# Mixture-of-experts weights: four split feature blocks and one plain fp32 block stationary, the rest streaming in pieces of 256, and a ring of ten weight tiles

## The chip, the cores and the metric

The kernel runs on one core of a Trainium2 chip. The metric is the device time of one execution in microseconds, as the median of several runs; lower is better. The core has a matrix engine (TensorE: PE in the profile, its weight loads PEld), a vector engine (VectorE, DVE), an activation engine (ScalarE, ACT), a general engine (GpSimd, POOL), a queue engine (SyncE, SP) that issues most transfers, and 16 DMA engines. Each engine runs its own instructions in order; engines wait for each other by semaphores. TensorE writes to PSUM, which DVE and ACT read.

A matmul on TensorE has two operands. The stationary one is loaded into the array first, with as many columns as the output has partitions; the moving one streams through it column by column. In the profile's rows a matmul reads `out<-moving,stationary`.

## The reference, cut to what matters

Two layers of a hybrid encoder. Each ends in a mixture of experts: 16 experts, each of which takes its 66 tokens of 528 (D_MODEL = 1024, EXPERT_FF = 1408). All of it is float32.

```python
def expert_choice_ffn(u, router, w1, w3, w2):
    B, L, D = u.shape
    cap = EC_FACTOR * L // N_EXPERTS
    aff = jax.nn.softmax(jnp.einsum("bld,de->ble", u, router).astype(jnp.float32), axis=-1)
    gates, idx = lax.top_k(jnp.swapaxes(aff, 1, 2), cap)
    xs = jax.vmap(lambda ub, ib: ub[ib])(u, idx)
    hid = jax.nn.silu(jnp.einsum("becd,edf->becf", xs, w1)) * jnp.einsum("becd,edf->becf", xs, w3)
    ys = jnp.einsum("becf,efd->becd", hid, w2) * gates[..., None].astype(u.dtype)
    return jax.vmap(lambda yb, ib: jnp.zeros((L, D), yb.dtype).at[ib].add(yb))(ys, idx)
```

## The kernel before

Everything ahead of the experts (input projection, three head groups, output projection, routing) is the same in both kernels. The change lies in the experts' stage, which runs once per layer.

**Weights.** Per expert, w1, w3 and w2 each come as four tiles of 128 partitions x 2816 (1408 KB); 12 tiles per expert, 384 in the program. `wtile` (L1100 issues it on SP) takes tiles from a ring of RA + RB = 9: five in one pool, four in another. A slot is loaded again when its last reader is through. One manual dependence holds a tile of the first fill back until the first expert's tokens are gathered.

**Split precision.** The fast matmul format fp32r doesn't keep all of float32, so each operand is split in a high and a low part, and three products are summed: high x high, low x high, high x low. `halve` splits a stretch of a weight tile: ACT copies it to fp32r (`wh`, L1111), DVE subtracts to get the rest (`wl`, L1112). Both land in rings of four buffers, so the splitting engines can be up to four pieces ahead of TensorE. For w1 and w3 a piece is one k: 128 rows of the weight matrix times all 1408 features, 8 pieces each. For w2 a tile is cut in two pieces of 1280 or 1536.

**Up (w1, w3).** `up_tile` (matmuls at L1156) multiplies one piece. Features 0 to 1023 stream as two stretches of 512 with the 66 tokens stationary, three matmuls each, into `h1a`/`h1b` (w3: `h3a`/`h3b`). Features 1024 to 1407 are three blocks of 128 that are stationary themselves; the tokens stream, high and low side by side (132 columns) against `wh` and high alone (66) against `wl`, into `h1T`/`h3T`. The wide and the short matmuls are issued in turn.

**Gate, down, order.** `gate_up` and `gated` form silu(w1 x) * (w3 x) on DVE and ACT, `hidden` transposes the row part back with eight TensorE transposes (`pth`) and splits it; `down` (L1217) streams w2 in stretches of 512 or 256 into `py`, `yo` scales by the gate (L1221), and an indirect DMA adds it into `hbuf` (L1222). `operands` transposes the next expert's tokens (`ptx`, eight transposes) and splits them (`xx`). The loop is a software pipeline: w1 of expert e, then w2 of expert e-1, then w3 of expert e; `hidden` of the previous expert follows the first tile of w1, `operands` of the next the second tile of w3. A scheduler orders each engine's instructions from this; the order within an engine is fixed when the program is built.

Of the kernel before, what the change touches and what calls it, by code (L numbers as in the profile page):

```python
# [23 lines left out]
D = 1024  # L24
# [22 lines left out]
RA, RB = 5, 4  # L47
WT = 2816

# [56 lines left out]
def body(ctx: ExitStack, tc: tile.TileContext, a, out, dbg=None, depth=DEPTH, stop=None):  # L106
# [104 lines left out]
    for l in range(depth):  # L211
# [879 lines left out]
        with tc.tile_pool(name="mw", bufs=1, reuse_waits="tile") as mw, \  # L1091
# [15 lines left out]
            def halve(w, lo, hi):  # L1107
                n = hi - lo
                wh = mhl.tile([128, 1536], F32R, name="wh", bufs=4)[:, :n]
                wl = mhl.tile([128, 1536], F32R, name="wl", bufs=4)[:, :n]  # L1110
                A.activation(wh, w[:, lo:hi], AF.Copy)  # L1111
                splits.append(behind(V.tensor_sub(wl, w[:, lo:hi], wh.bitcast(F32)),  # L1112
                                     chosen if len(splits) < 4 else None))
                return wh, wl

            def tokens(e):
                xg = mo.tile([128, D], F32, name="xg", bufs=3)
# [6 lines left out]
            def operands(xg):  # L1124
                xx = mo.tile([128, KT, 2, CAP], F32R, name="xx")
                for q in range(2):
# [6 lines left out]
                    A.activation(xx[:, ks, 0], src, AF.Copy)  # L1133
                    V.tensor_sub(xx[:, ks, 1], src, xx[:, ks, 0].bitcast(F32))  # L1134
                return xx

            def up_tile(src, xx, ps_, q):
# [20 lines left out]
            def halves(pT):  # L1158
                return pT[:, :6 * CAP].rearrange("p (b x n) -> p b n x", b=3, x=2)

            def gate_up(ps_):
                pa, pb, pT = ps_
                tt = mo.tile([128, 1024], F32, name="tt")
                tT = mo.tile([128, 2, 3, CAP], F32, name="tT")
                V.tensor_reduce(tT[:, 0], halves(pT), axis=AX.X, op=OP.add)
                for c, p in ((0, pa), (1, pb)):
                    t_ = tt[:CAP, c * 512:(c + 1) * 512]
                    A.activation(t_, p[:CAP, :], AF.Tanh, scale=0.5)
                    V.scalar_tensor_tensor(t_, t_, 1.0, p[:CAP, :], op0=OP.add, op1=OP.mult)
                A.activation(tT[:, 1], tT[:, 0], AF.Tanh, scale=0.5)  # L1170
                V.scalar_tensor_tensor(tT[:, 0], tT[:, 1], 1.0, tT[:, 0], op0=OP.add, op1=OP.mult)
                return tt, tT

            def gated(ts, ps_):
                (tt, tT), (pa, pb, pT) = ts, ps_
                for c, p in ((0, pa), (1, pb)):
                    t_ = tt[:CAP, c * 512:(c + 1) * 512]
                    V.tensor_mul(t_, t_, p[:CAP, :])
                V.tensor_reduce(tT[:, 1], halves(pT), axis=AX.X, op=OP.add)
                V.tensor_mul(tT[:, 0], tT[:, 0], tT[:, 1])  # L1180

            def hidden(ts):
# [3 lines left out]
                for c in range(3):  # L1186
                    if c < 2:
# [160 lines left out]
```

## Time and profile before

| what | value |
|---|---|
| device time, median of 3 runs | 2734.44 us (2730.94 to 2737.09) |
| profiled execution | 2737.51 us, its span 2735.7 us |
| busy over the span | PE 2518.9 us (92%), DVE 2170.6 (79%), ACT 1604.4 (59%), POOL 441.3 (16%) |
| weight tiles of the experts | 384 of 1408 KB, median 10.9 us from issue to landing |
| experts' stage | about 640 to 1355 us and 1985 to 2705 us |

The page cuts the span in 40 slices; in the two stretches of the experts' stage PE, DVE and DMA stand at 9 (90% or more) in every slice and ACT at 8. Elsewhere no engine is full for long. So the stage is read by itself: by windows of one expert, by the start times of TensorE's matmuls, and by groups of instructions that keep shapes apart. A matmul's duration includes its way through the array and overlaps the next one, so spacing is taken from start to start.

### The profile page before, as it was taken

How to read it: one execution, taken by the hardware profiler on the slowest of the kernel's cores; microseconds unless marked ns; L12 is line 12 of the kernel's file. 1: busy time of each engine (PE TensorE's matmuls, PEld its weight loads, DVE VectorE, ACT ScalarE, POOL GpSimd, SP SyncE). 2: the span in 40 equal slices, each digit the busy share in tenths (PEclk: the TensorE clock that was granted, in tenths of full speed). 3: DMA queues.
4: the chain of work that ended last, by engine and by line, in shares of the span. 5: the costliest groups of instructions: out<-in, count | busy, mean ns of one | idle time of the engine just before them, and what ended most of it. 6: DMA issues, size and time to landing. Idle time of an engine off the chain costs nothing.

```text
span 2735.7 us, 46610 instructions
## 1 busy us (share of the span) xinstructions
PE 2518.9 (92%) x18586; PEld 1981.8 (72%) x18586; DVE 2170.6 (79%) x3293; ACT 1604.4 (59%) x2107; POOL 441.3 (16%) x545
## 2 busy tenths in 40 slices
PE   7899999786999999999788899998689999999995
PEld 6778786565777777778587787755467787877783
DVE  3557667758999999999735676687589999999995
ACT  3324334425888888788542343344268888888884
POOL 3113322213000000000121133241120000000000
PEclk9878999997999999999997789999889999999998
DMA  3101101148999999999420111022499999999993
GB/s 129 47 24 60 37 25 51 64 172 312 408 400 405 403 399 409 397 412 404 174 77 32 40 44 49 13 73 93 148 358 393 413 397 411 399 409 401 407 402 117
DMA packets 84682, 643.30 MB, mean 235 GB/s; under 512 B 12592, under 2 KB 13040, under 8 KB 35312
## 3 DMA queue, kind: packets, MB, share of 16 engines
q1 hardware_dynamic: 75936, 618.16, 57.0%
q0 software_dynamic: 8528, 22.15, 3.3%
q8 instruction: 146, 2.39, 0.4%
q14 instruction: 72, 0.59, 0.1%
HBM read 617.05 MB, written 19.40 MB: 233 GB/s over the span
## 4 chain that ended last, share of the span: by engine, by line
PE 41%; DVE 5%; issue 2%; ACT 2%; DMA 1%; POOL 0%; DVEq 0%; SPq 0%; ACTq 0%; POOLq 0%
PE py L1217 9%; PE pj L288 5%; PE h1a L1156 4%; PE h3a L1156 3%; PE h1b L1156 3%; PE h3b L1156 3%; PE h1T L1156 1%; PE h3T L1156 1%; PE po L1026 1%; PE po L730 1%; DMA hbuf<-yo,idx 1%; PE S L898 1%; PE pl L473 1%; PE up L307 1%; PE py L563 0%
## 5 line engine op out<-in xcount | busy, mean ns | idle before, releaser
L1112 DVE TENSOR_TENSOR wl<-w,wh 128x1408 fp32r<-128x1408 f32 (+2 forms) x768 | 1212.7, 1617 | 59.9 <-ACT wh L1111 35.3
L1111 ACT ACTIVATE wh<-w 128x1408 fp32r<-128x1408 f32 (+2 forms) x768 | 1042.7, 1378 | 196.9 <-PE py L1217 78.5
L1217 PE MATMUL py<-wh,hh 128*66 128x512 f32 (+1 forms) x768 | 289.2, 377 | 4.3 <-ACT hh L1197 4.3
L1217 PE MATMUL py<-wh,hl 128*66 128x512 f32 (+1 forms) x768 | 288.7, 376 | 0.8 <-DVE hl L1198 0.8
L1217 PE MATMUL py<-wl,hh 128*66 128x512 f32 (+1 forms) x768 | 288.4, 375 | 0.0
L1222 POOL DMA_INDIRECT hbuf<-yo,idx x32 | 54.9, 1714 | 1190.0 <-ACT yo L1221 1076.6
L1156 PE MATMUL h1a<-wh,xx 128*66 128x512 f32 x512 | 186.1, 414 | 1.1 <-DVE xx L1134 1.1
L1156 PE MATMUL h3a<-wh,xx 128*66 128x512 f32 x512 | 182.8, 408 | 0.0
L1156 PE MATMUL h1b<-wh,xx 128*66 128x512 f32 x512 | 176.3, 410 | 0.0
L1156 PE MATMUL h3b<-wh,xx 128*66 128x512 f32 x512 | 174.7, 407 | 0.0
L1156 PE MATMUL h1T<-xx,wh 128*128 128x132 f32 x768 | 172.1, 224 | 0.0
L1156 PE MATMUL h3T<-xx,wh 128*128 128x132 f32 x768 | 171.3, 223 | 0.0
L288 PE MATMUL pj<-uh,wh 128*128 128x264 f32 (+1 forms) x896 | 166.5, 314 | 5.2 <-ACT kS L344 5.0
L288 PE MATMUL pj<-ul,wh 128*128 128x264 f32 (+1 forms) x896 | 162.2, 313 | 0.0
L288 PE MATMUL pj<-uh,wl 128*128 128x264 f32 (+1 forms) x896 | 155.6, 303 | 0.0
L1217 PEld LDWEIGHTS py<-wh,hh 128*66 128x66 f32 x768 | 105.2, 137 | 64.1 <-ACT hh L1197 4.5
L1217 PEld LDWEIGHTS py<-wl,hh 128*66 128x66 f32 x768 | 105.1, 137 | 60.6 <-issue 1.0
L1156 PE MATMUL h1T<-xx,wl 128*128 128x66 f32 x768 | 148.9, 194 | 0.0
L1156 PEld LDWEIGHTS h3T<-xx,wh 128*128 128x128 f32 x768 | 146.6, 191 | 2.7
L1156 PEld LDWEIGHTS h1T<-xx,wh 128*128 128x128 f32 x768 | 148.3, 193 | 0.0
L1156 PE MATMUL h3T<-xx,wl 128*128 128x66 f32 x768 | 148.3, 193 | 0.0
L1217 PEld LDWEIGHTS py<-wh,hl 128*66 128x66 f32 x768 | 105.3, 137 | 59.1 <-DVE hl L1198 1.5
(444 smaller groups left out, 5061.9 us busy)
## 6 DMA issues: line engine op xcount, KB each, us to landing
w<-in_e_w SPq DMA_DIRECT2D x384, 1408.0 KB, 10.9
w<-in_w_in SPq DMA_DIRECT2D x56, 512.0 KB, 3.5
wo<-in_w_out SPq DMA_DIRECT2D x16, 512.0 KB, 3.5
h<-hbuf SPq DMA_DIRECT2D x12, 512.0 KB, 4.7
swp<-raw SPq DMA_DIRECT2D x64, 66.0 KB, 2.0
h<-in_x SPq DMA_DIRECT2D x8, 512.0 KB, 7.2
hbuf<-h SPq DMA_DIRECT2D x8, 512.0 KB, 2.8
ubuf<-u POOLq DMA_DIRECT2D x8, 512.0 KB, 4.6
```

Source lines behind the costliest of these rows:

```text
L288: T.matmul(p[:M, c, :HL], ww[:, k, :M], uu[:, k, c * HL:(c + 1) * HL], start=(n == 0), stop=(n == 23))
L307: T.matmul(p[:, c, :HL], lhsT, rhs[:, c * HL:(c + 1) * HL], start=True, stop=True)
L473: T.matmul(pl[:, b, :], flat(BC[m][:, jm[m]]), az[:, m].rearrange("p x q n -> p (x q n)"), start=True, stop=True)
L730: T.matmul(o_, qd[d][hc(h), j * CH:(j + 1) * CH], kv[hc(h), d, j, :], start=False, stop=(d == 1), tile_position=(32 * h, 64 * (h % 2)))
L898: behind(T.matmul(p[:R], qk[0, h][:, qo:qo + R], qk[1, h][:, c, NM:], start=True, stop=True), mark)
L1026: T.matmul(p[:R, c, :], mm[:, k, o:o + R], ww[:, k, c * 512:(c + 1) * 512], start=(n == 0), stop=(n == 23))
L1111: A.activation(wh, w[:, lo:hi], AF.Copy)
L1112: splits.append(behind(V.tensor_sub(wl, w[:, lo:hi], wh.bitcast(F32)), chosen if len(splits) < 4 else None))
L1156: T.matmul(o_, l_, r_, start=s0, stop=s1)
L1217: T.matmul(py[:CAP, c, d0:d0 + n], x[:, kk, :], ww[:, at0 - lo:at0 - lo + n], start=(kk == 0 and i_ == 0), stop=(kk == FK - 1 and i_ == 2))
L1222: G.indirect_dma_start(out=hbuf[:, :], out_offset=bass.IndirectOffsetOnAxis(ap=idx[:CAP, e:e + 1], axis=0), in_=yo[:CAP], in_offset=None, ...
```

## The change

- Features 0 to 767 stream (FROW = 768), in stretches of 256: three stretches, nine matmuls per piece where there were six of 512.
- Features 768 to 1279 are four stationary split blocks (there were three). One of them goes to the free half of `h1b`/`h3b`.
- Features 1280 to 1407 are one stationary block in plain fp32: the weight tile itself is the operand, not split, against unsplit tokens `xf` (two more ACT copies per expert). So a tile of w1 or w3 has a third reader, TensorE.
- `halve` splits 1280 columns per piece of w1 or w3. Its buffers are 1280 wide (1536 before), so a w2 tile is cut in three pieces (1024, 1024, 768) and not two.
- Within a piece short and wide matmuls still take turns; in the last piece the wide ones go first.
- The epilogues read one bank more: a reduce and two small operations more in `gate_up` and in `gated`. The row part has six blocks to transpose and not eight.
- The ring has ten tiles (RB = 5). `xg` has two buffers (three), `yo` one (two).

```diff
-RA, RB = 5, 4
+RA, RB = 5, 5
 WT = 2816
+FROW, FCOL = 768, 1280
+NT = (FF - FROW) // 128
+WSPL = FCOL
...
-                wh = mhl.tile([128, 1536], F32R, name="wh", bufs=4)[:, :n]
-                wl = mhl.tile([128, 1536], F32R, name="wl", bufs=4)[:, :n]
+                wh = mhl.tile([128, WSPL], F32R, name="wh", bufs=4)[:, :n]
+                wl = mhl.tile([128, WSPL], F32R, name="wl", bufs=4)[:, :n]
...
-                xg = mo.tile([128, D], F32, name="xg", bufs=3)
+                xg = mo.tile([128, D], F32, name="xg", bufs=2)
...
                     A.activation(xx[:, ks, 0], src, AF.Copy)
+                    A.activation(xf[:, ks], src, AF.Copy)
...
-                    wh, wl = halve(w, j * FF, (j + 1) * FF)
+                    wh, wl = halve(w, j * FF, j * FF + FCOL)
...
-                    for c, p in ((0, pa), (1, pb)):
+                    for c in range(FROW // 256):
+                        p = (pa, pb)[c // 2][:CAP, c % 2 * 256:c % 2 * 256 + 256]
                         for i, (x, ww) in enumerate(((0, wh), (1, wh), (0, wl))):
-                            rows.append((p[:CAP, :], xx[:, kk, x], ww[:, c * 512:(c + 1) * 512],
-                                         first and i == 0, last and i == 2))
-                    for b in range(3):
-                        f = slice(1024 + 128 * b, 1152 + 128 * b)
-                        cols.append((pT[:, b * 2 * CAP:(b + 1) * 2 * CAP], wh[:, f],
-                                     xx[:, kk].rearrange("p x n -> p (x n)"), first and b == 0, False))
-                        cols.append((pT[:, b * 2 * CAP:b * 2 * CAP + CAP], wl[:, f], xx[:, kk, 0], False, last and b == 2))
-                    for pair in zip(rows, cols):
+                            rows.append((p, xx[:, kk, x], ww[:, c * 256:c * 256 + 256],
+                                         first and i == 0 and c == 0, last and i == 2 and c == 1))
+                    for b in (0, 1, 2, 3) if first else (1, 2, 3, 0):
+                        f = slice(FROW + 128 * b, FROW + 128 + 128 * b)
+                        p, at0 = (pb, 256) if b == 0 else (pT, (b - 1) * 2 * CAP)
+                        cols.append((p[:, at0:at0 + 2 * CAP], wh[:, f],
+                                     xx[:, kk].rearrange("p x n -> p (x n)"), first and b < 2, False))
+                        cols.append((p[:, at0:at0 + CAP], wl[:, f], xx[:, kk, 0], False, last and b == 0))
+                    cols.insert(6, (pT[:, 6 * CAP:7 * CAP], w[:, j * FF + FCOL:(j + 1) * FF], xf[:, kk], False, last))
+                    for pair in zip(rows, cols) if last else zip(cols, rows):
...
-                    mid = WT // 2 // 512 * 512 + (512 if q % 2 == 0 else 256)
-                    for lo, hi in ((0, mid), (mid, WT)):
+                    cuts = (0, 1024, 2048, WT) if q % 2 == 0 else (0, 768, 1792, WT)
+                    for lo, hi in zip(cuts, cuts[1:]):
...
-                yo = mo.tile([128, D], F32, name="yo")
+                yo = mo.tile([128, D], F32, name="yo", bufs=1)
```

The order on TensorE within a piece of w1, before; a row is line, operation, `out<-moving,stationary` and output partitions x columns:

```order
L1156 MATMUL h1a<-wh,xx 66x512
L1156 MATMUL h1T<-xx,wh 128x132
L1156 MATMUL h1a<-wh,xx 66x512
L1156 MATMUL h1T<-xx,wl 128x66
L1156 MATMUL h1a<-wl,xx 66x512
L1156 MATMUL h1T<-xx,wh 128x132
L1156 MATMUL h1b<-wh,xx 66x512
L1156 MATMUL h1T<-xx,wl 128x66
```

And the last twelve matmuls of such a piece in the changed kernel:

```order
L1165 MATMUL h1T<-xx,wl 128x66
L1165 MATMUL h1a<-wh,xx 66x256
L1165 MATMUL h1T<-xx,wh 128x132
L1165 MATMUL h1a<-wh,xx 66x256
L1165 MATMUL h1T<-xx,wl 128x66
L1165 MATMUL h1a<-wl,xx 66x256
L1165 MATMUL h1T<-xf,w 128x66
L1165 MATMUL h1b<-wh,xx 66x256
L1165 MATMUL h1b<-xx,wh 128x132
L1165 MATMUL h1b<-wh,xx 66x256
L1165 MATMUL h1b<-xx,wl 128x66
L1165 MATMUL h1b<-wl,xx 66x256
```

Each wide matmul still has a short one ahead of it; the seventh row is the new plain fp32 matmul, which reads the weight tile.

On DVE at the end of w1 and the start of w2, before (`wl` rows are splits, 1408 wide for w1, 1536 or 1280 for w2):

```order
L1112 TENSOR_TENSOR wl<-w,wh 128x1408 x2
L1112 TENSOR_TENSOR wl<-w,wh 128x1536
L1112 TENSOR_TENSOR wl<-w,wh 128x1280 x2
L1169 SCALAR_TENSOR_TENSOR tt<-tt,h1a 66x512
L1165 TENSOR_REDUCE tT<-h1T 128x198
L1112 TENSOR_TENSOR wl<-w,wh 128x1536
L1169 SCALAR_TENSOR_TENSOR tt<-tt,h1b 66x512
L1171 SCALAR_TENSOR_TENSOR tT<-tT 128x198
L1112 TENSOR_TENSOR wl<-w,wh 128x1536
```

and in the changed kernel:

```order
L1115 TENSOR_TENSOR wl<-w,wh 128x1280 x2
L1115 TENSOR_TENSOR wl<-w,wh 128x1024 x2
L1115 TENSOR_TENSOR wl<-w,wh 128x768
L1171 TENSOR_REDUCE tT<-h1T 128x198
L1184 SCALAR_TENSOR_TENSOR tt<-tt,h1a 66x512
L1169 TENSOR_REDUCE tT<-h1b 128x66
L1188 SCALAR_TENSOR_TENSOR tT<-tT,h1T 128x66
L1115 TENSOR_TENSOR wl<-w,wh 128x768
L1184 SCALAR_TENSOR_TENSOR tt<-tt,h1b 66x256
L1187 SCALAR_TENSOR_TENSOR tT<-tT 128x264
L1115 TENSOR_TENSOR wl<-w,wh 128x1024 x4
```

Four small operations now stand between the third and the fourth split of w2, where there were two.

On SP at the first fill of the ring, layer 0, before (numbers tell the tiles apart; DMASW is the gather of the first tokens):

```order
L1100 DMA w_7029<-in_e_w3 128x2816 [waits PE_49]
L1100 DMA w_7078<-in_e_w3 128x2816 [waits DMAHW4_49,Pool_49]
L1100 DMA w_7205<-in_e_w1 128x2816 [waits DVE_49]
L1100 DMA w_7112<-in_e_w3 128x2816 [waits DMAHW6_49,DMASW6_49]
L1100 DMA w_7153<-in_e_w1 128x2816 [waits DMAHW7_49]
```

and in the changed kernel:

```order
L1103 DMA w_7095<-in_e_w3 128x2816 [waits PE_49]
L1103 DMA w_7159<-in_e_w3 128x2816 [waits DMAHW4_49,Pool_49]
L1103 DMA w_7205<-in_e_w3 128x2816
L1103 DMA w_7260<-in_e_w1 128x2816 [waits DMAHW6_49,DMASW6_49]
L1103 DMA w_7322<-in_e_w1 128x2816 [waits DMAHW7_49]
```

The third of these tiles waited for DVE to split a first tile; it now waits for nothing and is issued with the two ahead of it. The next one still waits for the gather.

## Rows read from the trace of the kernel before

**Rows 1.** Windows: length, busy time (instructions) of PE, PEld, DVE, ACT, POOL, clock, DMA share, GB/s
```profile
921.55:965.78 44.23, 44.23 (x281) 34.41 (x280) 42.90 (x38) 35.97 (x34) 2.97 (x2) 1.00 1.01 406
1173.00:1217.00 44.00, 44.00 (x281) 34.28 (x280) 42.66 (x38) 35.75 (x34) 1.72 (x1) 1.00 1.01 411
```

**Rows 2.** Timeline of PE, one expert: start us, us, what, shape, count
```profile
921.55 0.40 PE L1156 MATMUL h3a<-wh,xx 128*66 128x512 f32 x1
...
928.51 0.69 PE L1129 MATMUL ptx<-cst,xg 66*128 66x66 f32 x8
929.00 0.43 PE L1156 MATMUL h3a<-wh,xx 128*66 128x512 f32 x1
...
950.50 0.42 PE L1217 MATMUL py<-wh,hh 128*66 128x512 f32 x1
...
965.78 0.39 PE L1156 MATMUL h3a<-wh,xx 128*66 128x512 f32 x1
```

**Rows 3.** Timeline of PE within a piece of w1
```profile
900.12 0.22 PE L1156 MATMUL h1T<-xx,wh 128*128 128x132 f32 x1
...
900.42 0.19 PE L1156 MATMUL h1T<-xx,wl 128*128 128x66 f32 x1
900.45 0.42 PE L1156 MATMUL h1b<-wh,xx 128*66 128x512 f32 x1
900.71 0.22 PE L1156 MATMUL h1T<-xx,wh 128*128 128x132 f32 x1
```

**Rows 4.** Timeline of PE in w2: last of 512 columns, first of six of 256
```profile
909.54 0.39 PE L1217 MATMUL py<-wl,hh 128*66 128x512 f32 x1
909.77 0.28 PE L1217 MATMUL py<-wh,hh 128*66 128x256 f32 x1
...
910.48 0.40 PE L1217 MATMUL py<-wh,hh 128*66 128x512 f32 x1
```

**Rows 5.** Plain fp32 elsewhere: L1049 by source, then timelines of PEld and PE
```profile
L1049 PE MATMUL plg<-rt,hT x160: 176/262/263, 548.8 to 1968.0; 128*128 128x16 f32 x128, 128*16 128x16 f32 x32
...
271.97 0.19 PEld L288 LDWEIGHTS pj<-ul,wh 128*128 128x128 f32 x1
272.07 0.98 PEld L550 LDWEIGHTS pu<-xs,zz 128*128 128x128 f32 x8
...
272.19 1.00 PE L550 MATMUL pu<-xs,zz 128*128 128x64 f32 x8
...
273.66 0.33 PE L557 MATMUL pS<-uv,bct 128*64 128x64 f32 x2
```

**Rows 6.** Groups by shape, 921.55 to 965.78, DVE then ACT: busy us, mean ns
```profile
L1112 DVE TENSOR_TENSOR wl<-w,wh 128x1408 fp32r<-128x1408 f32 x17 | 27.2, 1620 | 1.3 <-PE h3T L1156 0.6 <-ACT wh L1111 0.4
L1112 DVE TENSOR_TENSOR wl<-w,wh 128x1280 fp32r<-128x1280 f32 x4 | 5.8, 1482 | 0.0
...
L1133 ACT ACTIVATE xx<-ptx 128x264 fp32r<-128x264 f32 x2 | 0.7, 378 | 0.0
```

**Rows 7.** Timeline, fourth split of a w2: its DVE end, its first matmul
```profile
909.03 1.74 DVE L1112 TENSOR_TENSOR wl<-w,wh 128x1536 fp32r<-128x1536 f32 x1
...
911.86 0.39 PE L1217 MATMUL py<-wh,hh 128*66 128x512 f32 x1
```

**Rows 8.** Weight tiles by source, 700 to 1275: landing after issue
```profile
DMA to landing us min/median/max: 8.4/11.0/15.0
```

**Rows 9.** Timeline at the stage's start: first gather, first transposes
```profile
627.75 6.10 POOL L1118 DMA_INDIRECT xg<-ubuf,idx  x1 [4.38 <-DVE idx L1078]
...
637.69 1.14 PE L1129 MATMUL ptx<-cst,xg 66*128 66x66 f32 x8 [11.15 <-DMA xg<-ubuf,idx]
```

**Rows 10.** Timeline of PE, two fp32r streams before plain fp32 on 64 rows
```profile
89.51 0.40 PE L288 MATMUL pj<-uh,wh 128*128 128x264 f32 x2
89.90 0.31 PE L697 MATMUL pk<-vtC,km 64*32 64x64 f32 x7
```

More of the change, by code (lines that the diff above doesn't have):

```diff
@@ L1125, in operands @@
                 xx = mo.tile([128, KT, 2, CAP], F32R, name="xx")
+                xf = mo.tile([128, KT, CAP], F32, name="xf")
                 for q in range(2):
@@ L1133, in operands, with up_tile @@
                     A.activation(xx[:, ks, 0], src, AF.Copy)
+                    A.activation(xf[:, ks], src, AF.Copy)
                     V.tensor_sub(xx[:, ks, 1], src, xx[:, ks, 0].bitcast(F32))
-                return xx
-            def up_tile(src, xx, ps_, q):
+                return xx, xf
+            def up_tile(src, xs_, ps_, q):
+                xx, xf = xs_
                 w = wtile(src)
@@ L1155, in up_tile, with gathered @@
+                    cols.insert(6, (pT[:, 6 * CAP:7 * CAP], w[:, j * FF + FCOL:(j + 1) * FF], xf[:, kk], False, last))
+                    for pair in zip(rows, cols) if last else zip(cols, rows):
                         for o_, l_, r_, s0, s1 in pair:
                             T.matmul(o_, l_, r_, start=s0, stop=s1)
-            def halves(pT):
-                return pT[:, :6 * CAP].rearrange("p (b x n) -> p b n x", b=3, x=2)
-            def gate_up(ps_):
[L1162 to L1171, printed above, removed]
+            def gathered(dst, ps_):
+                pa, pb, pT = ps_
+                V.tensor_reduce(dst[:, 0], pb[:, 256:256 + 2 * CAP].rearrange("p (x n) -> p n x", x=2),
+                                axis=AX.X, op=OP.add)
+                V.tensor_reduce(dst[:, 1:4], pT[:, :6 * CAP].rearrange("p (b x n) -> p b n x", b=3, x=2),
+                                axis=AX.X, op=OP.add)
+                return pT[:, 6 * CAP:7 * CAP]
@@ new lines, in rows_of @@
+            def rows_of(ps_):
+                return ((slice(0, 512), ps_[0][:CAP, :]), (slice(512, FROW), ps_[1][:CAP, :FROW - 512]))
+            def gate_up(ps_):
+                tt = mo.tile([128, FROW], F32, name="tt")
+                tT = mo.tile([128, 2, NT, CAP], F32, name="tT")
+                own = gathered(tT[:, 0], ps_)
+                for c, p in rows_of(ps_):
+                    A.activation(tt[:CAP, c], p, AF.Tanh, scale=0.5)
+                    V.scalar_tensor_tensor(tt[:CAP, c], tt[:CAP, c], 1.0, p, op0=OP.add, op1=OP.mult)
+                A.activation(tT[:, 1, :4], tT[:, 0, :4], AF.Tanh, scale=0.5)
+                A.activation(tT[:, 1, 4], own, AF.Tanh, scale=0.5)
+                V.scalar_tensor_tensor(tT[:, 0, :4], tT[:, 1, :4], 1.0, tT[:, 0, :4], op0=OP.add, op1=OP.mult)
+                V.scalar_tensor_tensor(tT[:, 0, 4], tT[:, 1, 4], 1.0, own, op0=OP.add, op1=OP.mult)
@@ L1172, in gate_up @@
                 return tt, tT
             def gated(ts, ps_):
[L1175 to L1180, printed above, removed]
+                tt, tT = ts
+                for c, p in rows_of(ps_):
+                    V.tensor_mul(tt[:CAP, c], tt[:CAP, c], p)
@@ L1182, in hidden @@
+                own = gathered(tT[:, 1], ps_)
+                V.tensor_mul(tT[:, 0, :4], tT[:, 0, :4], tT[:, 1, :4])
+                V.tensor_mul(tT[:, 0, 4], tT[:, 0, 4], own)
             def hidden(ts):
@@ L1185, in hidden @@
                 hl = mo.tile([128, FK, CAP], F32R, name="hl")
-                for c in range(3):
-                    if c < 2:
+                for k0, n in ((0, 4), (4, 2), (6, NT)):
+                    if k0 < 6:
                         pt = t_tile("pth")
-                        for k in range(4):
-                            kk = 4 * c + k
-                            T.transpose(pt[:, k * CAP:(k + 1) * CAP], tt[:CAP, kk * 128:(kk + 1) * 128],
+                        for k in range(n):
+                            T.transpose(pt[:, k * CAP:(k + 1) * CAP], tt[:CAP, (k0 + k) * 128:(k0 + k + 1) * 128],
                                         ident[:CAP, :CAP])
-                        src = pt[:, :4 * CAP].rearrange("p (k n) -> p k n", k=4)
+                        src = pt[:, :n * CAP].rearrange("p (k n) -> p k n", k=n)
                     else:
                         src = tT[:, 0]
-                    ks = slice(4 * c, min(4 * c + 4, FK))
+                    ks = slice(k0, k0 + n)
                     A.activation(hh[:, ks, :], src, AF.Copy, scale=0.5)
```

## The prediction

> **What bounds the kernel now.** I read the windows of the experts' stage first, then TensorE's order of time, then what the other engines leave free. Over one expert, 921.55 to 965.78 us, PE is busy for all 44.23 us at a granted clock of 1.00 (the upper level, 2.4 GHz), DVE for 42.90, ACT for 35.97, and the DMA share is 1.01 [rows 1]. Four numbers near the limit, so a busy share alone doesn't decide. What decides is that PE's own spacing adds up to the period without a gap [rows 2]: w3 and w1 take 950.50 - 921.55 = 28.95 us, of which two blocks of eight transposes take 0.49 each (`ptx` in the rows, `pth` in w1 alike), so sixteen pieces (one piece: the 128 rows of one k times all 1408 features) take 27.97, or 1.748 us each; the w2 matmuls take 965.78 - 950.50 = 15.28. Together 44.23. TensorE is the bound, and a change is worth what it takes out of PE's spacing, as long as DVE (1.33 us free per expert) and the DMA queue can follow. There are 512 pieces in the kernel (16 for each of 32 experts).
>
> **TensorE, one piece.** Ends of matmuls are modelled, so I use start to start. Before, a piece is six pairs of a 512-column matmul and a short one (132 or 66 columns), 0.29 a pair: from 900.12 to 900.42 and on to 900.71 [rows 3]; 1.748/6 = 0.291. In the w2 stream a 512-column matmul takes 0.230 and six of 256 take 0.71, so 0.118 each [rows 4]: time goes by columns, nothing fixed is lost by halving. So of a pair 0.230 is the wide stream and 0.061 the short one with the loads that aren't hidden. After, eight pairs have a 256-column stream: 8 x (0.118 + 0.061) = 1.432.
>
> The ninth pair holds the plain fp32 matmul (`h1T<-xf,w`). The trace has plain fp32 with 128 stationary columns elsewhere: each of the program's matmuls leaves two records (160 for the 2 x 5 x 8 of L1049) [rows 5]. Eight such records with 64 moving columns, L550, have loads 0.113 apart (eight in 0.98, one lasts 0.19: 0.79/7), though by their columns they would stream faster: the load of 128 stationary columns sets the pace [rows 5]. The first of the two loads hides behind the 256-column stream before it (0.118 against 0.113, so barely); the second doesn't. The pair costs 0.113 + 0.061 + 0.118 = 0.29. Bounds: 0.18, an ordinary pair, if both loads hide; 0.40 if neither does. I take 0.29, since L550 is the same shape but for two columns.
>
> So a piece becomes 1.432 + 0.292 = 1.724 by the pairs. If the short halves follow the streams and loads alone (0.059 and 0.118), it is 8 x 0.177 + 0.290 = 1.706. I take 1.716: 0.032 saved, 16.4 us over 512 pieces. With the far bounds of the fp32 pair a piece lies between 1.61 and 1.84, so 70 us saved or 47 lost.
>
> A rule speaks against this. The Trainium skill, TensorE: Matmul & The Clock Gate, section Back-to-back issue gap, gives a sustained spacing of about 131 ns a matmul at 512 columns and 81 at 128. By it a piece would go from 6 x 131 + 6 x 81 = 1.27 us to 9 x 98 + 10 x 81 = 1.69 (estimates from that page, 98 on a straight line), and the kernel would lose 215 us where the rows give a gain of 16. The trace has 230 and 118 ns [rows 4], so the rule doesn't hold here at 512 columns.
>
> **Other edits on TensorE.** Hidden activations are transposed in six blocks per expert where there were eight: two times 0.49/8 = 0.061, so 0.12 per expert, 3.9 us. The w2 matmuls keep their number and widths (the new cuts lie on the same 512 boundaries); only the pieces they wait for shrink.
>
> **DVE and ACT, hidden now, and what if not.** Splits of w1 and w3 shrink from 1408 to 1280 columns: 1620 to 1482 ns on DVE [rows 6]; sixteen times 0.138 is 2.2 us less per expert. Of w2, 8 pieces become 12. By the slope of these two rows (1.08 ns a column, 0.10 fixed) the four extra starts cost 0.4. The row and column epilogues gain a reduce and two small operations each and lose 256 columns: about +0.6. So DVE goes from 42.9 to about 41.5 in a period of 43.6. ACT gains four starts and two copies of 264 columns (0.38 each [rows 6]), loses 16 x 0.1: hidden in its 8.3 free us. The order shows the one tight place: at the end of w1 DVE does four small operations between two w2 splits where it did two. Before, the fourth w2 split ends at 909.03 + 1.74 = 910.77 and PE starts on that piece at 911.86 [rows 7], 1.1 us early. After, splits are 0.3 us per piece cheaper against PE's pace, the block 0.4 longer, the pieces shorter: I get 0.4 to 1.1 early. Nothing, then; if that cover is gone, 0.3 us in 30 experts, 9 us.
>
> **The ring.** A tile of w1 or w3 is now also read by PE, so it comes free when PE has passed it and not when DVE has split it: about 2.5 us later (DVE's lead, 1.1, plus the piece). The tenth tile gives 3.7 back. A slot turned round in 9 x 44.23/12 = 33.2 us, of which 11.0 in flight [rows 8] and some 5 in work (two splits of 1.6 and the copy ahead of them), so about 17 us of tiles lie ready. That cushion matters, since with a DMA share of 1.01 the queue may not be able to go faster than 44.2 per expert. It would be drained by 0.6 us per expert, 8 us over the 13 experts with gathers, less than 17; once gathers stop the queue moves more, 411 GB/s [rows 1]. So I expect no starving. The Trainium skill, DMA: Bandwidth & Descriptors, Specifications, puts the ceiling at 435 GB/s; an estimate from it is 40 us for an expert's twelve tiles, and by that the first rival below would have no chance. The trace shows 406 GB/s at a share of 1.01 [rows 1], so I keep it.
>
> **Start of the stage.** Before, the first gather (627.75) shares the queues with a weight tile that SP issues when a first tile comes free; ptx then sits 11.15 us behind the gather [rows 9]. In the new order that tile has no wait and goes out with the ones before, so the gather is alone. Between 0 and 2 us per layer; I take 0.5, 1 us in all.
>
> **Sum.** 16.4 + 3.9 + 1.0 = 21.3 us. The profiled execution took 2737.5 us (span 2735.7 and 1.8 around it), 3.1 over the median; the difference carries over: 2734.4 - 21.3 = 2713 us.
>
> **Rivals.**
> First, the queue takes over: PE is quicker but the cushion isn't there, because tiles are held longer. For: share 1.01, and 11.0 us to landing, three tiles deep [rows 1, 8]. Against: 17 us ready. If a third of the cushion can be used, 5 us per layer and 2 more once gathers end: 2720; if none, 2734. I take 2727, chance 0.12.
> Second, DVE's longer epilogue delays PE by 0.3 us per expert: 2722, chance 0.08.
> Third, on the slow side: short matmuls carry a fixed price. A transpose of 66 columns takes 0.061, while a 66-column matmul in the stream advances by 0.03 (900.42 to 900.45) [rows 2, 3], so 0.031 each might be fixed. A piece has seven records more: 0.22 us, 111 over the kernel, 2824. Against: 512 and 256 columns take 0.230 and 0.118 [rows 4]. The Trainium skill's spacing (section Back-to-back issue gap, above) is such a price. It decides from 6 ns per added record. Chance 0.03.
> Fourth, also slower: PE pauses on going between fp32r and plain fp32. Two streams of 264 columns before L697 last 0.39, where 0.118 for 256 columns makes 0.24 [rows 10]: 0.15 more, 512 times is 77 us, 2790. Against: L697 works on 64 rows, and around L550, on all 128, eight records and four streams of 264 take 273.66 - 272.19 = 1.47 [rows 5], where 8 x 0.113 + 4 x 0.12 = 1.38. It decides from 41 ns per piece. Chance 0.09.
> Fifth, both fp32 loads hide: the piece falls to 1.61, DVE (41.5) and the cushion stop it at about 17 us per layer: 2700. Chance 0.05.
>
> **How the numbers follow.** My forecast, 2705 to 2722, has 0.60; 0.03 is for what I don't see. Range 2700 to 2736: it holds forecast, queue and DVE cases and leaves out the two slow rivals and the fast edge. A measurement here tells apart about 0.2%, or 5.5 us. Faster: forecast, DVE, fifth rival and half of the queue case, 0.78; the same, 0.10; slower, 0.12.
>
> **What would show it.** A period of 43.5 to 43.7 with PE still gapless; starts 0.18 apart in ordinary pairs; two records for `xf` 0.11 apart; DVE at about 41.5; landing times that grow through a layer. Wrong: PE idle before a `wh` or `wl` (DVE, ACT or the queue), an `xf` pair over 0.33, or 256-column starts above 0.125 in the pieces.

## The result and the profile after

The changed kernel takes 2710.02 us (median of 4 runs, 2707.35 to 2713.18) where the kernel before took 2733.12 beside it (4 runs, 2730.94 to 2737.09): a ratio of 0.9914, 95% interval 0.9897 to 0.9931. A second measurement, five runs, gave 2714.52 against 2734.41, ratio 0.9921 (0.9906 to 0.9936). The forecast was 2713 in a range from 2700 to 2736. The total came out as forecast. The sum behind it did not: its largest term is too large by 6.5 us, and three terms are missing from it.

The window over one expert answers to [rows 1]: length, then busy time (instructions) of PE, PEld, DVE, ACT and POOL, clock, DMA share, GB/s.

```profile
918.51:962.26 43.75, 43.75 (x391) 38.12 (x390) 41.77 (x46) 35.34 (x40) 3.08 (x2) 1.00 1.01 401
```

TensorE still runs without a gap at a granted clock of 1.00, in 43.75 us where it took 44.23. DVE is busy for 41.77 (42.90 before), the DMA share is the same. The timeline of PE (start, duration, line, matmul, shape, count) answers to [rows 2]:

```profile
918.54 0.22 PE L1165 MATMUL h3b<-xx,wh 128*128 128x132 f32 x1
...
925.40 0.66 PE L1133 MATMUL ptx<-cst,xg 66*128 66x66 f32 x8
925.86 0.31 PE L1165 MATMUL h3T<-xx,wh 128*128 128x132 f32 x1
...
947.00 0.42 PE L1233 MATMUL py<-wh,hh 128*66 128x512 f32 x1
...
962.30 0.23 PE L1165 MATMUL h3b<-xx,wh 128*128 128x132 f32 x1
```

w3 and w1 take 947.00 - 918.54 = 28.46 us (28.95 before), w2 15.30 (15.28). The transposes take 0.46 (`ptx`) and 0.34 (`pth`, 936.27 to 936.61), so sixteen pieces take 27.66, 1.729 each. Inside a matrix a piece is shorter than that. Here is one of w1, answering to [rows 3]:

```profile
897.33 0.31 PE L1165 MATMUL h1a<-wl,xx 128*66 128x256 f32 x1
897.48 0.33 PE L1165 MATMUL h1T<-xf,w 128*128 128x66 f32 x2
897.62 0.31 PE L1165 MATMUL h1b<-wh,xx 128*66 128x256 f32 x1
...
898.12 0.23 PE L1165 MATMUL h1T<-xx,wh 128*128 128x132 f32 x1
...
898.48 0.23 PE L1165 MATMUL h1T<-xx,wh 128*128 128x132 f32 x1
...
899.19 0.33 PE L1165 MATMUL h1T<-xf,w 128*128 128x66 f32 x2
```

From one `xf` to the next is 899.19 - 897.48 = 1.71. Two ordinary pairs take 898.48 - 898.12 = 0.36, 0.18 each. The plain fp32 pair, from the wide start ahead of it to the next, takes 897.62 - 897.33 = 0.29, with two records. Its loads, in the rows of PEld:

```profile
897.36 0.31 PEld L1165 LDWEIGHTS h1T<-xf,w 128*128 128x128 f32 x2
```

A single load of 128 columns lasts 0.19 there, so the second of the two starts 0.12 behind the first.

Where the 24.3 us between the two profiled executions lie (spans 2735.7 and 2711.4), read from the starts of TensorE's first and last matmul of each stretch:

| stretch | before, us | after, us | difference |
|---|---|---|---|
| to the first `ptx`, layer 1 | 637.69 | 637.39 | -0.30 |
| experts of layer 1, to the last `py` | 716.02 | 706.33 | -9.69 |
| last `py` to the first transpose of layer 2 | 17.51 | 15.69 | -1.82 |
| layer 2 from there to its first `ptx` | 622.46 | 618.64 | -3.82 |
| experts of layer 2 | 715.54 | 706.75 | -8.79 |
| last `py` to the end | 26.5 | 26.6 | +0.1 |

In a layer fifteen periods are shorter by 0.46 us each, 7 us. The other 2.7 and 1.8 us of the two experts' stages are what the last expert gained, less 0.7 that the first expert of layer 2 lost. In the last expert w2 has no next expert's work beside it, and TensorE waits for its operands; the bracket is the idle time and what ended it. Before, then after:

```profile
1336.44 0.45 PE L1217 MATMUL py<-wh,hh 128*66 128x512 f32 x1 [2.13 <-ACT hh L1197]
1337.30 0.45 PE L1217 MATMUL py<-wh,hl 128*66 128x512 f32 x1 [0.41 <-DVE hl L1198]
...
1338.81 0.63 PE L1217 MATMUL py<-wh,hh 128*66 128x512 f32 x1
1339.24 0.63 PE L1217 MATMUL py<-wh,hl 128*66 128x512 f32 x1
```

```profile
1328.43 0.44 PE L1233 MATMUL py<-wh,hh 128*66 128x512 f32 x1 [1.61 <-ACT hh L1213]
...
1330.11 0.40 PE L1233 MATMUL py<-wh,hh 128*66 128x512 f32 x1
1330.35 0.39 PE L1233 MATMUL py<-wh,hl 128*66 128x512 f32 x1
```

Before, matmuls of 512 columns start 0.43 apart for some 3.4 us; after, 0.23 to 0.24, as everywhere. The window over those 3.4 us gives the reason in the clock, the figure behind POOL's, before and after:

```profile
1338.00:1341.40 3.40, 3.40 (x10) 1.77 (x9) 0.00 (x0) 1.48 (x1) 0.24 (x1) 0.52 0.54 77
```

```profile
1330.00:1333.40 3.40, 3.40 (x20) 2.28 (x19) 2.06 (x2) 2.91 (x3) 0.00 (x0) 1.00 0.53 80
```

The granted clock was 0.52, the lower of its two levels (1.2 GHz) for nearly all of the stretch, after two waits of 2.13 and 0.41 us; after one of 1.61 it stayed at 1.00. The last expert's w2 took 17.27 and 17.25 us in the two layers before, 15.29 and 15.35 after. With the shorter wait that is 2.5 and 2.4 us.

Between the layers the two queues show this, before and then after:

```profile
1354.84 2.34 POOL L203 TENSOR_TENSOR wl<-w,wh 128x1024 fp32r<-128x1024 f32 x1 [16.60 <-ACT wh L202]
1357.37 1.48 POOL L1222 DMA_INDIRECT hbuf<-yo,idx  x1 [0.18 <-DMA lam_p<-in_df_lam]
...
1363.79 2.21 SPq L196 DMA_DIRECT2D h<-hbuf  x5
```

```profile
1345.56 1.48 POOL L1238 DMA_INDIRECT hbuf<-yo,idx  x1 [7.96 <-ACT yo L1237]
...
1351.74 2.22 SPq L199 DMA_DIRECT2D h<-hbuf  x5
```

Before, the last expert's scatter stood on POOL behind a weight split of the next layer, 3.7 us behind the last `py` (1353.71); after, it goes first, 1.8 us behind (1343.72). The load of `h` follows 6.2 to 6.4 us later in both.

### The profile page after: what moved, and what is told of

Read it like the earlier page. It is cut to its first block, busy times and chain, and to the rows that moved or that the text cites. A ratio compares the mean times of both kernels' runs of the same rounds, so it can differ in the third digit from the quotient of the medians.

```text
span 2711.4 us, 54579 instructions
## 1 busy us (share of the span) xinstructions
PE 2501.7 (92%) x22106; PEld 2103.4 (78%) x22106; DVE 2133.4 (79%) x3549; ACT 1583.9 (58%) x2331; POOL 432.5 (16%) x545
## 4 chain that ended last, share of the span: by engine, by line
PE 79%; DVE 11%; issue 4%; ACT 3%; DMA 1%; POOL 0%; SPq 0%; DVEq 0%; ACTq 0%; POOLq 0%
PE py L1233 17%; PE pj L291 10%; PE h1a L1165 8%; PE h3a L1165 7%; PE h1b L1165 5%; PE h3b L1165 5%; PE h1T L1165 4%; PE h3T L1165 4%; PE po L1029 2%; PE po L733 1%; PE S L901 1%; PE pl L476 1%; PE py L566 1%; PE po L731 1%; PE pq L501 1%
## 5 line engine op out<-in xcount | busy, mean ns | idle before, releaser
L1115 DVE TENSOR_TENSOR wl<-w,wh 128x1280 fp32r<-128x1280 f32 (+2 forms) x896 | 1160.8, 1334 | 79.2 <-ACT wh L1114 66.9
L1114 ACT ACTIVATE wh<-w 128x1280 fp32r<-128x1280 f32 (+2 forms) x896 | 1008.2, 1148 | 201.1 <-PE h3b L1165 70.5
L1238 POOL DMA_INDIRECT hbuf<-yo,idx x32 | 64.2, 2008 | 1188.2 <-ACT yo L1237 1078.0
L1165 PE MATMUL h1a<-wh,xx 128*66 128x256 f32 x1024 | 243.9, 297 | 0.0
L1165 PE MATMUL h3a<-wh,xx 128*66 128x256 f32 x1024 | 241.5, 294 | 0.0
L1165 PE MATMUL h1a<-wl,xx 128*66 128x256 f32 x512 | 152.1, 297 | 0.0
L1165 PE MATMUL h3a<-wl,xx 128*66 128x256 f32 x512 | 151.1, 295 | 0.0
```

The source lines that it names most:

```text
L1165: T.matmul(o_, l_, r_, start=s0, stop=s1)
L1238: G.indirect_dma_start(out=hbuf[:, :], out_offset=bass.IndirectOffsetOnAxis(ap=idx[:CAP, e:e + 1], axis=0), in_=yo[:CAP], in_offset=None, ...
```

## Experiments

**The changed kernel again**, unedited.

> The changed kernel once more, beside the others of this group, so that they can be compared on one chip. If the period of an expert (43.76 us against 44.23 before) carries the gain alone, 32 experts give 15 us; the profiled executions differ by 24.3. My theory puts the rest at the ends of the experts' stage: 2.6 us per layer around the last expert's w2 (TensorE waits 1.6 us for its operands where it waited 2.1 and 0.4, and the granted clock stays at 1.00 where it fell to about 0.52 for 3.4 us), 1.8 us once between the layers, 1 us per layer at the first gather; I expect about 2710 again, and these four places again. The rival is that the 9 us beside the period are spread of single executions: then this run's profile shows them at other places.

2714.52 us, ratio 0.9921 (0.9906 to 0.9936). The same places again: period 43.78, the last w2 15.30 and 15.36, 16.07 between the layers, 8.9 us from gather to transposes in both layers. So the places are the kernel's and not the spread of one execution. Whether the clock stays up at the last w2 is another matter: two executions don't settle it, and the runs below show it falling behind the same wait.

**Seams.** The average piece (1.729) is longer than one inside a matrix (1.71): in each expert the three pieces behind a seam (the start of w1 and the pieces behind the two blocks of transposes) take 1.79 to 1.82. In the changed kernel a matrix ends in a short matmul and the next begins with one:

```profile
932.73 0.19 PE L1165 MATMUL h3b<-xx,wl 128*128 128x66 f32 x1
932.76 0.30 PE L1165 MATMUL h1b<-xx,wh 128*128 128x132 f32 x1
932.90 0.28 PE L1165 MATMUL h1a<-wh,xx 128*66 128x256 f32 x1
```

From the short start at 932.76 to the next start is 0.14; a short start that follows a wide one has the next 0.06 behind it. The edit begins every pair with the wide one:

```
-                    for pair in zip(rows, cols) if last else zip(cols, rows):
+                    for pair in zip(rows, cols):
```

> The changed kernel, but each pair of a piece begins with its wide matmul (256 columns) in every piece, not only in the last of a matrix. Theory 1, seams: a piece inside a matrix now repeats after 1.71 us as forecast, but where a piece begins with a short matmul behind another short one or behind transposes, the second load of 128 columns has nothing to hide behind, and the next start comes 0.14 us later where it comes 0.06 later elsewhere; two or three such places per expert (w3 to w1, behind ptx, behind pth) make 0.15 to 0.24. Then the period falls from 43.76 to 43.5 to 43.6 and the kernel is 5 to 8 us faster than the changed one: about 2703 to 2705. Theory 2: the seams come from the change of matrix and of PSUM banks, whatever the order: period 43.76, no change. Theory 3: the DMA queue (share 1.01) already holds the period at 43.76: the seams vanish from TensorE's order of time, but waits for tiles take their place, and the time stays at 2710.

The same place, edited:

```profile
928.95 0.20 PE L1165 MATMUL h3b<-xx,wl 128*128 128x66 f32 x1
928.98 0.31 PE L1165 MATMUL h1a<-wh,xx 128*66 128x256 f32 x1
929.13 0.22 PE L1165 MATMUL h1b<-xx,wh 128*128 128x132 f32 x1
929.19 0.28 PE L1165 MATMUL h1a<-wh,xx 128*66 128x256 f32 x1
```

Wide, short, wide follow each other as inside a matrix, and the period falls to 43.66. That is 0.11, of the 0.15 to 0.24 expected: the seam costs what was said, but the transposes, which had started the next load early, now take 0.51 and 0.39 where they took 0.46 and 0.34. No wait for a tile took the place of the seams, so the queue doesn't hold the period at 43.76. The time is 2710.06 (ratio 0.9916, 0.9901 to 0.9931), not 2703 to 2705: 3.6 us in the periods, but in this profile the clock fell behind the last expert's wait in both layers (16.92 and 16.87 us for that w2). The wait itself is the same 1.61 us as in the changed kernel.

**The price of the fp32 pair, and what bounds next.** The plain fp32 matmul is left out of six of eight pieces:

```
-                    cols.insert(6, (pT[:, 6 * CAP:7 * CAP], w[:, j * FF + FCOL:(j + 1) * FF], xf[:, kk], False, last))
+                    cols.insert(6, (pT[:, 6 * CAP:7 * CAP], w[:, j * FF + FCOL:(j + 1) * FF], xf[:, kk], False, last)
+                                if first or last else None)
...
-                        for o_, l_, r_, s0, s1 in pair:
+                        for o_, l_, r_, s0, s1 in filter(None, pair):
```

> The changed kernel with the plain fp32 matmul left out of six of the eight pieces of w1 and of w3 (the fifth block's sum lacks those six). It prices the fp32 pair and asks what bounds next. Theory of loads: the step from one matmul to the next takes the longer of its own stream and the next one's load of stationary columns (0.113 for 128 of them, about 0.06 for 66); without its two records a piece loses 0.113 and 0.061, from 1.71 to 1.54 inside a matrix. Rival, a pause between fp32r and plain fp32 hidden in the 0.29: more than 0.174 goes, a piece falls below 1.50. Rival, both loads hide: about 0.06 goes. For the period: 12 of 16 pieces lose 0.174, so TensorE alone would need 41.7 us where it needs 43.76. If only TensorE bounds, the period falls to about 41.8 (DVE is busy for 41.8 too) and the kernel takes about 2650; if the DMA queue is already at its limit (share 1.01), TensorE gets waits for wh or wl once the cushion is used up and the period stays near 43.5: about 2700.

```profile
741.64 0.22 PE L1166 MATMUL h3T<-xx,wh 128*128 128x132 f32 x1
...
743.18 0.22 PE L1166 MATMUL h3T<-xx,wh 128*128 128x132 f32 x1
```

A piece without it repeats after 1.54 us: 0.17 less, which is one load of 128 columns in the open and one short step, as priced. A hidden pause would have made the difference larger, two hidden loads would have made it 0.06. The time is 2693.22 (ratio 0.9845, 0.9823 to 0.9867), between the two cases given for the period, because it has two phases. Windows of about one period, early and late in the first layer, then landing times of weight tiles from 700 to 800 and from 900 to 1000 us:

```profile
746.13:788.00 41.87, 41.87 (x370) 36.05 (x368) 41.36 (x46) 35.10 (x40) 3.34 (x2) 1.00 1.01 408
...
1089.00:1139.00 50.00, 44.14 (x370) 38.21 (x369) 41.47 (x46) 35.22 (x41) 3.34 (x2) 0.93 1.01 407
```

```profile
DMA to landing us min/median/max: 14.0/18.4/22.0
```

```profile
DMA to landing us min/median/max: 27.0/30.3/31.6
```

For the first experts the period is 41.8, with landing times that rise from expert to expert. When they reach 30 us the tiles that lay ready are used up, and the next four periods are 43.98, 45.56, 43.87 and 49.98, with TensorE idle in them. In the last of them ACT waits up to 7.9 us for a tile to land, DVE 7.6 for ACT, and TensorE 5.9 for DVE. The next bound is the DMA queue: over the layer a period averages 43.15 us.

**Pieces of 512.** The 768 streaming columns go as 512 and 256, with two short matmuls behind each of 512. Every pair begins with its wide matmul here too, so the kernel to compare with is the one with the wide matmul first, whose period is 43.66:

```
-                    for c in range(FROW // 256):
-                        p = (pa, pb)[c // 2][:CAP, c % 2 * 256:c % 2 * 256 + 256]
+                    for c, n in ((0, 512), (2, 256)):
+                        p = (pa, pb)[c // 2][:CAP, :n]
...
-                    for pair in zip(rows, cols) if last else zip(cols, rows):
-                        for o_, l_, r_, s0, s1 in pair:
+                    for i in range(3):
+                        rows.insert(2 * i + 1, None)
+                    for pair in zip(rows, cols):
+                        for o_, l_, r_, s0, s1 in filter(None, pair):
```

> The changed kernel with the 768 streaming columns in pieces of 512 and 256 instead of three of 256: three matmuls fewer in a piece; behind each wide one of 512 stand two short ones, behind each of 256 one. Theory of loads (a step takes the longer of its stream and the next load): a group of 512, short, short takes 0.230 + 0.113 + 0.061 = 0.404, one of 256 and a short 0.179, the one with plain fp32 0.292; a piece takes 3 x 0.404 + 2 x 0.179 + 0.292 = 1.86 where it takes 1.71, the period 46.1, the kernel about 2787. Rival, columns alone decide: no change, 2710. Rival, each matmul has a fixed price of 0.03: three fewer make 0.09 less per piece, 42.3, and the kernel is up to 40 us faster.

The matmuls of a piece, then three loads of its first group:

```profile
902.37 0.42 PE L1167 MATMUL h1a<-wh,xx 128*66 128x512 f32 x1
902.62 0.22 PE L1167 MATMUL h1T<-xx,wh 128*128 128x132 f32 x1
902.68 0.24 PE L1167 MATMUL h1T<-xx,wl 128*128 128x66 f32 x1
902.76 0.43 PE L1167 MATMUL h1a<-wh,xx 128*66 128x512 f32 x1
...
904.22 0.58 PE L1209 MATMUL pth<-cst,tt 66*128 66x66 f32 x6
```

```profile
902.39 0.19 PEld L1167 LDWEIGHTS h1T<-xx,wh 128*128 128x128 f32 x1
902.63 0.19 PEld L1167 LDWEIGHTS h1T<-xx,wl 128*128 128x128 f32 x1
902.74 0.14 PEld L1167 LDWEIGHTS h1a<-wh,xx 128*66 128x66 f32 x1
```

A group takes 902.76 - 902.37 = 0.39 to 0.41 (0.404 expected), a piece 904.22 - 902.37 = 1.85 (1.86 expected). The period is 45.88, the time 2777.86, ratio 1.0155 (1.0134 to 1.0176): slower than the kernel before, with three matmuls fewer in every piece. So neither columns alone nor a fixed price per matmul describe this stream. What does, in the group and in the piece, is the sum of steps that are each the longer of a matmul's own stream and the next one's load. The loads show it step by step: they start 0.24 apart, then 0.11 (0.230 and 0.113 by that count). The starts of the matmuls bear it out in their sum alone, standing 0.25, 0.06 and 0.08 apart. And columns alone don't price a load: the transposes, whose stationary operand has 128 columns on 66 rows, follow each other at 0.06 [rows 2]. The Trainium skill, TensorE: Matmul & The Clock Gate, section Back-to-back issue gap, has spacings of about 131 ns at 512 columns and 81 at 128; by an estimate from it (98 at 256) three of 512 for six of 256 would save 0.2 us per piece, where this run lost 0.14.

**The ring.** Nine tiles for ten (`RA, RB = 5, 4`) in the changed kernel.

> The changed kernel with nine weight tiles in the ring, as before. Theory: the cushion of tiles that lie ready is large enough, so the period stays at 43.76, and only the start of the stage loses what the tenth tile gave there (about 1 us per layer: the first transposes come 10 us behind the gather's start where it is 8.8 now): 1 to 3 us slower than the changed kernel. Rival, the queue: the cushion of nine isn't enough for tiles that are held until TensorE has passed them; then TensorE waits for tiles late in the stretch with gathers, and the time is 5 us per layer slower, 2720.

2711.75 us, ratio 0.9918 (0.9902 to 0.9933), period 43.78, no wait for a tile, and the first transposes still 8.71 and 8.91 us behind the gather. The tenth tile isn't needed, neither for the period nor for the gain at the start, which this run's expectation had put down to it.

**The start of the stage.** From the first gather to the first transposes it was 9.94 and 10.52 us before (two layers), 8.85 and 8.80 after. Three things differ there. The first is read from the traces: DVE's splits of the first tiles, before and then after, with the first gather on POOL after (the one before is in [rows 9]):

```profile
626.75 6.22 DVE L1112 TENSOR_TENSOR wl<-w,wh 128x1408 fp32r<-128x1408 f32 x4
```

```profile
627.54 5.68 DVE L1115 TENSOR_TENSOR wl<-w,wh 128x1280 fp32r<-128x1280 f32 x4
...
628.54 5.57 POOL L1121 DMA_INDIRECT xg<-ubuf,idx  x1 [4.38 <-DVE idx L1081]
```

The gather's instruction ends 0.9 us behind the last of the four splits in both, and 0.88 or 0.89 behind it in both layers of all twelve kernels. The next gather, with DVE idle, lasts 0.95. The splits are narrower by 128 columns now, and the gather is done in 5.57 us instead of 6.10 (5.62 for 6.14 in layer 2): 0.5 us per layer. What holds it is not shown.

The other two are the tile that waits for DVE among the first ones (in the order before, not with nine or ten tiles in the changed kernel), and a third gather, since the change also takes the buffers for gathered tokens from three to two. The gather is edited alone, first in the kernel before:

```
-                xg = mo.tile([128, D], F32, name="xg", bufs=3)
+                xg = mo.tile([128, D], F32, name="xg", bufs=2)
```

> The kernel before with two buffers for gathered tokens instead of three, nothing else: only two gathers are issued ahead of the first transposes where there were three, and the weight tile that waits for DVE stays. From the first gather's start to the first transposes the kernel before took 9.94 and 10.52 us in its two layers, the changed kernel 8.85 and 8.80. Theory 1, the third gather shares the queue with the first: here too it falls to 8.8 to 9.0. Theory 2 (the prediction's), the tile that goes out when DVE has split a first one lands among the gather's rows: it stays at 9.9 to 10.5. In either case the period stays at 44.24, and the time within 3 us of the kernel before.

9.45 and 10.81 us, within the 9.34 to 10.81 that the four kernels with the old order show. 2737.80 us, ratio 1.0009 (1.0000 to 1.0019). Then in the changed kernel:

```
-RA, RB = 5, 5
+RA, RB = 5, 4
-                xg = mo.tile([128, D], F32, name="xg", bufs=2)
+                xg = mo.tile([128, D], F32, name="xg", bufs=3)
```

> The changed kernel with nine weight tiles and three buffers for gathered tokens: the third gather is back, the tile that waits for DVE ahead of the gather's tiles isn't. Theory 1 (third gather): from the first gather to the first transposes 9.9 to 10.5 us again, where the changed kernel with nine tiles and two buffers took 8.7 and 8.9. Theory 2 (the tile): it stays at 8.7 to 9.0. Period 43.78 either way, time 2710 to 2714.

9.01 and 9.09 us, within the 8.59 to 9.44 of the eight kernels with the new order. 2712.76 us, ratio 0.9924 (0.9908 to 0.9941). So the third gather doesn't decide. On average over the kernels the new order is 0.8 us shorter in the first layer and 1.6 in the second, of which the splits make 0.5. What is left, 0.2 and 1.0, may be the tile's place in SP's order, as the prediction said; no run moves that tile alone, and from the end of the gather's instruction to the transposes the two orders overlap (3.2 to 4.7 us and 3.0 to 3.8).

**The last expert's w2.** First the cuts alone, in the kernel before:

```
-                    for lo, hi in ((0, mid), (mid, WT)):
+                    cuts = (0, 1024, 2048, WT) if q % 2 == 0 else (0, 768, 1792, WT)
+                    for lo, hi in zip(cuts, cuts[1:]):
```

> The kernel before with w2 split in three pieces a tile (1024, 1024, 768 columns) instead of two, nothing else. Theory: in steady state nothing changes (period 44.23). In the last expert of a layer the operands of its w2 are made behind a split on ACT and DVE; with pieces of 768 and 1024 for 1536 these come earlier (ACT 0.84 for 1.48, DVE 0.95 for 1.76 us), TensorE waits about 1.6 us in one stretch where it waited 2.1 and 0.4, and the clock stays at its upper level: 2 to 2.6 us per layer, 4 to 5 in all, about 2729. Rival: the shorter wait of the changed kernel comes from its own epilogue (768 row columns for 1024, six transposes for eight) and not from the cuts: then the wait here stays at 2 us or more, the clock falls to about 0.5 for 3 us as before, and the time is that of the kernel before.

2728.76 us, ratio 0.9983 (0.9972 to 0.9994), period 44.24 as before. The wait is one of 1.49 us, and the scatter stands ahead of POOL's split as in the changed kernel (15.79 us between the layers; in all kernels it is 14.3 to 16.1 with the new cuts and 17.2 to 18.0 with the old). So the shorter wait and the earlier scatter come from the cuts of w2 alone. The last w2 took 15.32 us in the first layer, but 16.89 in the second: there the clock fell all the same. The one shorter wait doesn't rule that out.

Then the clock alone: in the kernel before TensorE is kept busy through the wait.

```
+                if e == NE - 1:
+                    fill = sm_tile("fill")
+                    for _ in range(12):
+                        T.matmul(fill[:CAP, :6 * CAP], xx[:, 0, 0], xx[:, 0:3].rearrange("p k x n -> p (k x n)"),
+                                 start=True, stop=True)
                 py = py_tile("py")
```

> The kernel before, with twelve extra matmuls of 396 columns (about 2.1 us, into a PSUM bank that nobody reads) in TensorE's wait ahead of the last expert's w2, in each layer. Theory: the 17.25 us that this w2 takes against 15.28 elsewhere come from the granted clock, which is at 0.52 for 3.4 us after TensorE has waited there. With TensorE busy through the first wait the clock stays at 1.00, this w2 takes 15.3 to 15.8 (0.4 of waiting for hl is left), and each layer ends 1.5 to 2 us earlier: about 3 to 4 us, 2731. Rival: the slow matmuls are short of something else there (their pieces, or the port that reads them); then they stay at 0.43 apart, and the time is that of the kernel before or up to 0.3 us worse per layer.

```profile
1333.90 2.36 PE L1207 MATMUL fill<-xx 128*66 128x396 f32 x12
1336.23 0.45 PE L1222 MATMUL py<-wh,hh 128*66 128x512 f32 x1
1337.09 0.45 PE L1222 MATMUL py<-wh,hl 128*66 128x512 f32 x1 [0.41 <-DVE hl L1198]
```

```profile
1337.50:1340.90 3.40, 3.40 (x19) 2.17 (x18) 0.42 (x1) 1.58 (x2) 0.53 (x1) 1.00 0.50 63
```

The operands come when they came before, the 0.41 us wait is still there, and the clock stays at 1.00. This w2 takes 15.68 us in both layers (17.27 and 17.25 without). 2731.71 us, ratio 0.9983 (0.9971 to 0.9994): 3.6 us by the medians; these two places make 3.2 in the profiles.

Last, both finds on the changed kernel: the wide matmul first, and ten such matmuls ahead of the last w2.

> The changed kernel with each pair's wide matmul first, and with ten extra matmuls of 396 columns (about 1.8 us, into a bank that nobody reads) ahead of the last expert's w2 in each layer, where TensorE waits 1.6 us for its operands. The order alone gave a period of 43.66, but in that run's profile the clock fell behind this wait in both layers, to about 0.55, and the last w2 took 16.9 us. Theory: with TensorE busy there the clock stays up, the last w2 takes 15.3 to 15.5 in both layers, and the kernel comes to 2706 or 2707, 3 to 5 us under the changed one. Rival: the clock falls all the same, or the extra matmuls delay w2 by as much as they save: 2710.

Period 43.66, the last w2 15.33 in both layers at a granted clock of 1.00. 2707.82 us, ratio 0.9899 (0.9881 to 0.9917), the fastest of the complete kernels. Its lead over the changed one (ratio 0.9914 and 0.9921) is within the intervals; what is shown is the shorter period and the two undisturbed ends.

## Why the prediction was right, point by point

**The bound.** Right: TensorE sets the period before and after, with no gap in either.

**The piece.** Its mechanism was right to a hundredth: pairs of 0.18, the plain fp32 pair at 0.29 with the second load in the open (0.12 behind the first, 0.11 forecast), 1.71 for a piece inside a matrix (1.716 taken). The step that failed is "16.4 us over 512 pieces". It took the piece inside a matrix, 1.716, for all sixteen and carried no seam. Before, no piece is longer than 1.77 and the average is 1.748; after, the three behind a seam take 1.79 to 1.82. In the run with the wide matmul first the average is 1.717. By the averages it is 1.748 - 1.729 = 0.019, or 0.31 per expert, 9.9 us in 32. The order had shown the place: the matrix before begins with a wide matmul everywhere, the changed one with a short one. I had read it for DVE and SP only.

**Transposes.** 0.18 per expert for 0.12, 5.8 us for 3.9. But a part of it is the load that the short matmul behind them starts early and pays for at the seam: with the wide one first they take 0.90 together, and 0.08 is left of the gain.

**The start.** 1.1 and 1.7 us per layer, where 0.5 was taken from 0 to 2. The forecast read 11.15 as the distance from the gather to the transposes; that is TensorE's idle time, and the distance is 9.94 [rows 9]. Its cause, the tile's place, is a part at most: 0.5 us per layer comes with the narrower splits, which it had costed for the steady state only.

**DVE.** A group by shape, 918.51 to 962.26, and the fourth split of a w2 with TensorE's start on its piece, answering to [rows 6, 7]:

```profile
L1115 DVE TENSOR_TENSOR wl<-w,wh 128x1280 fp32r<-128x1280 f32 x17 | 24.8, 1486 | 1.2 <-ACT wh L1114 0.8
```

```profile
904.74 0.95 DVE L1115 TENSOR_TENSOR wl<-w,wh 128x768 fp32r<-128x768 f32 x1
...
907.11 0.28 PE L1233 MATMUL py<-wh,hh 128*66 128x256 f32 x1
```

41.77 us per period for 41.5 (the forecast's own terms add up to 41.7), and the fourth split ends at 905.69, 1.4 us ahead of TensorE (0.4 to 1.1 forecast). It is hidden, so the second rival fell.

**The queue.** Landing times, which were 9.1/10.9/13.6 from 700 to 800 us before and 10.2/13.0/15.0 from 1100 to 1200, are these after, in the same two stretches:

```profile
DMA to landing us min/median/max: 8.5/11.6/14.1
```

```profile
DMA to landing us min/median/max: 17.6/19.1/22.5
```

They grow through the layer, as forecast, and the cushion lasts. The first rival's mechanism is real, as the run without the fp32 matmul shows. By the 43.15 us of that run it comes in when some 0.6 us more are taken from the period (an estimate).

**The other rivals.** The fixed price per short matmul and the pause between fp32r and plain fp32 fell with the runs on wide pieces and without the fp32 pair. Both loads don't hide: 0.17, not 0.06.

**What the sum lacks.** The last expert of a layer (2.5 and 2.4 us) and the hand-over between the layers (1.8) follow from the cuts of w2, which the prediction costed at nothing outside the steady state. It looked at one expert in the middle and not at the last, where nothing covers a wait. Of the last experts' 4.9 us some 3.2 are the clock, which fell in both layers before and in neither after; in other kernels it fell behind the changed kernel's wait of 1.61 us too, so this part isn't sure in every execution. And layer 2 ahead of its experts ran 2.1 us shorter, beside 1.7 at its start of stage, in code that the change doesn't touch. In the other kernels the same stretch stood between 8.0 shorter and 1.5 longer than before, edits as small as one buffer among them (4.0 shorter). The instructions of DVE, ACT and POOL there stand in the same order, by name, in all of them, and two profiles of the changed kernel lie 0.4 us apart; what decides it stays open, and I put that part down to none.

So by the measured terms: periods 0.46 x 15 x 2 = 14, last experts 4.9, hand-over 1.8, starts 2.8 and layer 2 ahead of its experts 2.1 make 25.6; the rest, a loss of 1.3, lies in the first experts and in layer 1 ahead of its gather. That the forecast of 21.3 met it is luck: 6.5 us too much in one term stood against some 9 missing and two small terms that were too low.

## What to carry to other kernels

Cost a matmul stream step by step, as the longer of one matmul's stream and the next one's load, with both prices read from rows of the same shapes, and do it at the seams as well as inside: an order that alternates wide and short pays wherever two short ones meet. A change to a repeated stage is also a change to its last repetition, where the work that hid a wait is missing; read that one in the trace on its own. And when the total is as forecast, hold the terms against the trace all the same.

## What was not expected of the hardware

The granted clock can fall to its lower level behind a wait of TensorE as short as 1.5 to 1.6 us. After one such wait ahead of the last w2 it fell in 5 of 16 cases (the changed kernel and its variants without fill, and the kernel before with the new cuts, two layers each), after 2.13 and 0.41 us in 4 of 4, and with TensorE kept busy through the wait in 0 of 4. A fall cost 1.6 us each time: 16.9 us for this w2 instead of 15.3. The same program showed both: with nine tiles the clock fell in the first layer and not in the second, behind equal waits.

A gather on POOL ended with splits on DVE that it has no data in common with. The first gather's instruction lasted 5.6 us beside four splits of 1280 columns on DVE and 6.1 beside four of 1408, and ended 0.88 or 0.89 us behind the last of them in 24 of 24 cases; the next gather, with DVE idle, took 0.95 or 0.96. What links the two is not shown.
